# Low parts of the up-projection weights by an accumulating transfer instead of a VectorE subtraction, in a hybrid decoder layer on one core

## The chip, the cores and the metric

The kernel runs on one core of a Trainium2 chip. A core has a matrix engine (TensorE, PE in the profile; its weight loads are PEld), VectorE (DVE), ScalarE (ACT), GpSimd (POOL) and SyncE (SP), which here only issues transfers. Each engine works through its own list of instructions in order and waits on semaphores for the others. Sixteen DMA engines carry the transfers of all queues. On-chip data lie in SBUF (128 partitions), matmul results in PSUM (8 banks of 128 x 512 float32).

The metric is the device time of one execution in microseconds (us). The kernel before has a median of 772.62 us over 3 runs, from 772.52 to 773.3.

## The reference

One decoder layer on x of 512 x 1024, float32. Two attention branches (forgetting attention and stick-breaking attention, 8 heads each) are merged and projected; then comes a gated MLP with a causal convolution of width 3 between its up-projection and the gate. What the change touches is the up-projection of this second half:

```python
x = layer_norm(ALPHA * x + (1 + gt1) * attn_out, ln1_g, ln1_b)
u2 = x * (1 + sc2) + sh2
h = causal_depthwise_conv(u2 @ w_up, conv_w, conv_b)   # w_up: 1024 x 5632
h_gate, h_val = split(h, 2)
ffn_out = (silu(h_gate) * h_val) @ w_down              # w_down: 2816 x 1024
x = layer_norm(ALPHA * x + (1 + gt2) * ffn_out, ln2_g, ln2_b)
```

## The kernel before, in words

**Products in three parts.** TensorE is used with a reduced-precision float32 format (`F32R`). Each operand is split into a high part, the value rounded to that format, and a low part, the rounding error. A product is the sum of three matmuls: high x high, high weights x low activations, low weights x high activations (`mm3`, lines 110 to 112, in this order). The high part of a weight tile is a copy on ScalarE (`hi_of`, line 75, tile name `wh`), the low part is `raw - wh`, a subtraction on VectorE (`lo_of`, line 78, tile name `wl`).

**The stream of weight tiles.** All weights come as tiles of 128 x 1024 float32 (512 KB). `add_item` lists them with a function that prepares each; `weights(i)` issues the loads on SyncE's queue into four buffers called `raw`, up to three tiles ahead of i, and calls the preparing function up to two tiles ahead. For the up-projection that function is `split_proc` (line 143): it takes one of three `wh` and one of three `wl` buffers and makes the two parts. Four other kinds of tiles use the same four `raw` buffers: between the up tiles come 8 tiles `wa` of the conditioning weights, accumulated on VectorE (lines 524 and 529), and at the end the tiles `wdn` of the down-projection, which GpSimd first multiplies by the gate row `gt` (line 587).

**The up-projection.** Its 44 tiles are numbered n = 0 to 43 (gate and value columns alternate). For each, 8 groups of three matmuls fill one PSUM bank of 128 x 512. The first three tiles are done in two halves of 256 columns, because the second half of the activations is still being normalized. After a tile's matmuls ScalarE evacuates the bank with the convolution's last tap and bias (line 912, `cv`), VectorE adds the two other taps (lines 913, 914); after each odd tile ScalarE does the SiLU (line 919), VectorE the product (line 920), and the result is split into `hh` (ScalarE) and `hl` (VectorE).

**GpSimd during this stage.** From n = 6 on the code asks for `o_x1` (line 852), which finishes the first LayerNorm's output for the later residual: two rows are scaled by -0.5 (line 799, `lnr`) and 16 operations on 128 x 512 (lines 856 and 857, `xn`) multiply and add.

**What sets the order.** SyncE's instructions stand in the order of the program text. For the four other engines a scheduler orders the instructions when the kernel is built, by data dependences and by its own estimate of durations, and puts in the semaphore waits; on the chip each engine then keeps to its list.

Of the kernel before, what the change touches and what calls it, by code (L numbers as in the profile page):

```python
# [9 lines left out]
F32R = mybir.dt.float32r  # L10
BF16 = mybir.dt.bfloat16
AF = mybir.ActivationFunctionType
ALU = mybir.AluOpType
# [3 lines left out]
P = 128  # L17
# [18 lines left out]
WBUFS = 3  # L36
# [9 lines left out]
def layer_kernel(ctx: ExitStack, tc: tile.TileContext, out, xT, x, cT, crow, wa0, wa1, bcol, bgt, w1, wct, wv, bf,  # L46
# [3 lines left out]
    V, S, G, PE = nc.vector, nc.scalar, nc.gpsimd, nc.tensor  # L50

    cons = ctx.enter_context(tc.tile_pool(name="cons", bufs=1))
    stg = ctx.enter_context(tc.tile_pool(name="stg", bufs=1))
# [7 lines left out]
    def nm(s):  # L61
        cnt[0] += 1
        return f"{s}_{cnt[0]}"
# [7 lines left out]
    def fl(ap):  # L71
        return ap.bitcast(F32)

    def hi_of(o, i, scale=1.0):
        S.activation(o, i, AF.Copy, scale=scale)  # L75

    def lo_of(o, i, hi):
        return V.tensor_tensor(o, i, fl(hi), ALU.subtract)  # L78
# [39 lines left out]
    def add_item(src, proc, cols=1024):  # L118
        items.append([src, proc, cols, None, None])
        return len(items) - 1  # L120

    def weights(i, ahead=AHEAD):
        while state["load"] < min(len(items), i + LOADS):
            it = items[state["load"]]
            it[3] = stg.tile([P, 1024], F32, name=nm("raw"), tag="raw", bufs=LOADS)
            nc.sync.dma_start(it[3][:, 0 : it[2]], it[0])
            state["load"] += 1
            while state["proc"] <= state["load"] - LOADS:
                process()
        while state["proc"] < min(len(items), i + 1 + ahead):  # L130
            process()
        return items[i][4]
# [10 lines left out]
    def split_proc(r, cols=1024):  # L143
        h = stg.tile([P, 1024], F32R, name=nm("wh"), tag="wh", bufs=WBUFS)
        l = stg.tile([P, 1024], F32R, name=nm("wl"), tag="wl", bufs=WBUFS)
        hi_of(h[:, 0:cols], r[:, 0:cols])
        lo_of(l[:, 0:cols], r[:, 0:cols], h[:, 0:cols])
        return h, l


# [365 lines left out]
    def ada_proc(n):  # L516
        def f(r):
            if 8 <= n < 24:
                mod_col(2 + (n - 8) // 8, n % 8, r)
                return  # L520
            g, q = n // 4, n % 4
            if q == 0:
                ada_st[g] = z(F32, "ac2")
                V.tensor_scalar_mul(ada_st[g], r[:, 0:512], cTs[:, 0:1])
            acc = ada_st[g]
            for e in range(2):
                k = 2 * q + e
                if k > 0:
                    V.scalar_tensor_tensor(acc, r[:, e * 512 : (e + 1) * 512], cTs[:, k : k + 1], acc, ALU.mult, ALU.add)
        return f  # L530
# [54 lines left out]
    def wdn_proc(late):  # L585
        def f(r):
            G.tensor_tensor(r, r, gt[1], ALU.mult)  # L587
            if not late:
                h, l = split_proc(r)
                return [h[:, 0:512], h[:, 512:1024]], [l[:, 0:512], l[:, 512:1024]]  # L590
            h = [z(F32R, "wdh") for _ in range(2)]
            l = [z(F32R, "wdl") for _ in range(2)]
            for e in range(2):
                c = slice(e * 512, (e + 1) * 512)
                hi_of(h[e], r[:, c])
                lo_of(l[e], r[:, c], h[e])
            return h, l
        return f
# [20 lines left out]
    def add_proj(n, after):  # L619
        stream.append((proj, (add_item(wct[TILES.index(n)], split_proc), after)))  # L620
        flush_sum(len(stream))
# [7 lines left out]
    def add_bproj(br, j, after):  # L629
        if j % 2 == 0:  # L630
            wpi[br] = add_item(wp[br, j // 2], split_proc)
        stream.append((bproj, (br, j, wpi[br], after)))
# [227 lines left out]
    hh, hl = [], []  # L860
    wui, wai = [], {}
    for n in range(2 * FT):
        wui.append(add_item(wup[n], split_proc))
        if n % 4 == 3 and adas[0] < 32:
            add_item(wa1[adas[0]], ada_proc(adas[0]))
            wai[adas[0]] = len(items) - 1
            adas[0] += 1
# [27 lines left out]
    for n in range(2 * FT):  # L895
        if n < NSPLIT:
            h, l = items[wui[n]][4]
            ps = bks[n]
            up_mm(ps, h, l, slice(256, 512))
        else:  # L900
            ps = bank()
            h, l = weights(wui[n])
# [48 lines left out]
    for i in range(NB):  # L951
        tb = slice(i * P, (i + 1) * P)
        r = x1[i]
# [95 lines left out]
```

## The profile and times before

| | us |
|---|---|
| median of 3 runs | 772.62 |
| lowest, highest | 772.52, 773.3 |
| profiled execution, whole | 772.12 |
| its span in the trace | 770.3 |
| TensorE busy in the span | 748.1 (97%) |
| VectorE busy | 549.4 (71%) |
| ScalarE busy | 350.4 (45%) |
| GpSimd busy | 185.7 (24%) |
| up-projection, from the first matmul of tile 0 to the end of tile 43 | 400.2 to 642.4 |

The profile follows one execution. A row of a timeline gives start, duration, engine, line, operation, output and inputs, and in brackets how long the engine had been idle and who released it; a row with `x2` is two instructions merged. A row of groups gives after the bar the busy time, the mean duration in ns and the idle time before the instructions. A row of a window gives its length, then busy time and count of TensorE, weight loads, VectorE, ScalarE and GpSimd, then the granted clock, the DMA engines' share and GB/s. In the list of transfers the last number is the median time from issue to landing. Matmuls overlap in their pipeline, so each one's duration (0.39 us) is longer than the distance between two.

### The profile page before, as it was taken

Reading aid. Unit: us, or ns where it says so; the run is one execution under the profiler, and the core shown is the slowest. Engines: PE = TensorE matmul, PEld = TensorE weight load, DVE = VectorE, ACT = ScalarE, POOL = GpSimd, SP = SyncE. Lnnn points to the kernel's source line nnn. Section 1 sums busy time; section 2 is a strip of 40 time slices with the busy share of each in tenths; the row PEclk is TensorE's granted clock in tenths of the full one; section 3 lists DMA queues with packets and bytes.
Section 4 is the critical chain, followed back from the end, with each engine's and each line's share of the span. In section 5 each row is a group of like instructions: output and inputs, shape, how many; then the busy total and the mean of one; then the engine's idle time right before and its main releaser. Section 6 shows DMA issues by size and latency. Waiting matters only on the chain.

```text
span 770.3 us, 9560 instructions
## 1 busy us (share of the span) xinstructions
PE 748.1 (97%) x3556; PEld 620.6 (81%) x3556; DVE 549.4 (71%) x822; ACT 350.4 (45%) x583; POOL 185.7 (24%) x138
## 2 busy tenths in 40 slices
PE   5998999999999999999999999999999999999995
PEld 3886887788888888888889888888888888888885
DVE  6979889966687977776676787686656665533666
ACT  3357686717667556333145434444444433222400
POOL 1025424510000011364000780000000043945500
PEclk9999999999999999999999999999999999999998
DMA  8951253542333323455302524354332214323202
GB/s 310 403 204 55 83 165 131 175 161 83 110 110 110 127 93 136 144 190 164 137 1 73 201 79 145 118 177 137 114 105 93 100 55 165 120 98 127 65 28 83
DMA packets 31105, 99.68 MB, mean 129 GB/s; under 512 B 4273, under 2 KB 4785, under 8 KB 31058
## 3 DMA queue, kind: packets, MB, share of 16 engines
q1 hardware_dynamic: 30546, 99.00, 37.0%
q8 instruction: 28, 0.46, 0.2%
q14 instruction: 19, 0.16, 0.1%
q0 software_dynamic: 512, 0.07, 0.1%
HBM read 96.88 MB, written 2.10 MB: 128 GB/s over the span
## 4 chain that ended last, share of the span: by engine, by line
PE 86%; DVE 6%; ACT 5%; DMA 1%; issue 1%; SPq 0%; DVEq 0%; ACTq 0%
PE ps L110 17%; PE ps L111 17%; PE ps L112 17%; PE ps L941 5%; PE ps L940 5%; PE ps L942 5%; PE ps L254 4%; PE ps L495 2%; PE ps L821 2%; PE ps L820 2%; PE ps L819 2%; PE ps L477 2%; DVE om L456 1%; DMA wa<-in_wa 1%; ACT wh L75 1%
## 5 line engine op out<-in xcount | busy, mean ns | idle before, releaser
L78 DVE TENSOR_TENSOR wl<-raw,wh 128x1024 fp32r<-128x1024 f32 (+2 forms) x106 | 143.8, 1357 | 101.0 <-ACT wh L75 100.5
L75 ACT ACTIVATE wh<-raw 128x1024 fp32r<-128x1024 f32 (+2 forms) x106 | 110.4, 1042 | 108.1 <-PE ps L942 39.9
L110 PE MATMUL ps<-u2h,wh 128*128 128x512 f32 (+1 forms) x376 | 141.4, 376 | 0.0
L111 PE MATMUL ps<-u2l,wh 128*128 128x512 f32 (+1 forms) x376 | 141.2, 376 | 0.0
L112 PE MATMUL ps<-u2h,wl 128*128 128x512 f32 (+1 forms) x376 | 141.2, 375 | 0.0
L587 POOL TENSOR_TENSOR raw<-raw,gt 128x1024 f32<-128x1024 f32 x22 | 60.7, 2774 | 187.1 <-DVE gt L550 157.6
L110 PE MATMUL ps<-uh,wh 128*128 128x512 f32 x232 | 92.9, 400 | 2.2 <-DVE vv L78 2.2
L112 PE MATMUL ps<-uh,wl 128*128 128x512 f32 x232 | 90.8, 391 | 0.0
L111 PE MATMUL ps<-ul,wh 128*128 128x512 f32 x232 | 90.8, 391 | 0.0
L110 PEld LDWEIGHTS ps<-u2h,wh 128*128 128x128 f32 x376 | 70.8, 188 | 12.9
L111 PEld LDWEIGHTS ps<-u2l,wh 128*128 128x128 f32 x376 | 70.8, 188 | 12.8
L112 PEld LDWEIGHTS ps<-u2h,wl 128*128 128x128 f32 x376 | 70.8, 188 | 12.6
L110 PEld LDWEIGHTS ps<-uh,wh 128*128 128x128 f32 x232 | 43.6, 188 | 10.7 <-DVE vv L78 2.5
L112 PEld LDWEIGHTS ps<-uh,wl 128*128 128x128 f32 x232 | 43.6, 188 | 9.4
L111 PEld LDWEIGHTS ps<-ul,wh 128*128 128x128 f32 x232 | 43.7, 188 | 7.9
L940 PE MATMUL ps<-wh,hh 128*128 128x512 f32 x128 | 49.8, 389 | 0.0
L941 PE MATMUL ps<-wl,hh 128*128 128x512 f32 x128 | 49.8, 389 | 0.0
L942 PE MATMUL ps<-wh,hl 128*128 128x512 f32 x128 | 49.8, 389 | 0.0
L457 POOL TENSOR_TENSOR pt<-pt,om 128x127 f32<-128x127 f32 (+3 forms) x32 | 40.0, 1278 | 33.8 <-DVE om L456 28.7
L75 ACT ACTIVATE hh<-cv 128x512 fp32r<-128x512 f32 x22 | 13.9, 631 | 59.6 <-DVE cv L920 59.6
L575 POOL TENSOR_TENSOR raw<-raw,gt 128x1024 f32<-128x1024 f32 x8 | 21.1, 2645 | 78.0 <-DVE m L78 42.2
L919 ACT ACTIVATE cv<-cv 128x512 f32<-128x512 f32 x22 | 13.9, 632 | 54.5 <-DVE cv L914 54.5
(188 smaller groups left out, 1463.0 us busy)
## 6 DMA issues: line engine op xcount, KB each, us to landing
raw<-in_wup SPq DMA_DIRECT2D x44, 512.0 KB, 3.3
raw<-in_wa SPq DMA_DIRECT2D x32, 512.0 KB, 3.3
raw<-in_wct SPq DMA_DIRECT2D x29, 512.0 KB, 3.2
raw<-in_wdn SPq DMA_DIRECT2D x22, 512.0 KB, 3.2
wa<-in_wa SPq DMA_DIRECT2D x14, 512.0 KB, 8.7
raw<-in_wp SPq DMA_DIRECT2D x8, 512.0 KB, 3.3
raw<-in_wo SPq DMA_DIRECT2D x8, 512.0 KB, 3.6
raw<-in_w SPq DMA_DIRECT2D x7, 452.0 KB, 8.3
```

The costliest lines, as they stand in the source:

```text
L75: S.activation(o, i, AF.Copy, scale=scale)
L78: return V.tensor_tensor(o, i, fl(hi), ALU.subtract)
L110: PE.matmul(ps, wh, ah, start=first, stop=False)
L111: PE.matmul(ps, wh, al, start=False, stop=False)
L112: PE.matmul(ps, wl, ah, start=False, stop=last)
L254: PE.matmul(grp[g], w, u, start=j == 0 and n == 0, stop=j == KT - 1 and n == (1 if g == 7 else 2))
L457: G.tensor_tensor(pt[b][:, s : e - 1], pt[b][:, s : e - 1], om[:, s + 1 : e], ALU.mult)
L575: G.tensor_tensor(r, r, gt[0], ALU.mult)
L587: G.tensor_tensor(r, r, gt[1], ALU.mult)
L940: PE.matmul(ps, hh[j][:, tb], w[0], start=first, stop=False)
L941: PE.matmul(ps, hh[j][:, tb], w[1], start=False, stop=False)
L942: PE.matmul(ps, hl[j][:, tb], w[0], start=False, stop=last)
```

## The change

The 44 tiles of the up-projection are prepared by a new function, `split_dma`, in place of `split_proc`. ScalarE writes the negated high part into the `wl` buffer and the high part into the `wh` buffer, both from the raw tile. Then a transfer issued on GpSimd's queue adds the raw tile to what stands in `wl`, element by element, within SBUF. The result is `raw - high`, as before. VectorE's 44 subtractions are gone; ScalarE has 44 more copies, GpSimd's queue 44 transfers of 512 KB. A `raw` buffer of an up tile now comes free when the transfer has landed and the copies are done. TensorE's list and SyncE's list keep their order. All other tiles are split as before.

```diff
+    def split_dma(r):
+        h = stg.tile([P, 1024], F32R, name=nm("wh"), tag="wh", bufs=WBUFS)
+        l = stg.tile([P, 1024], F32R, name=nm("wl"), tag="wl", bufs=WBUFS)
+        hi_of(l, r, -1.0)
+        hi_of(h, r)
+        G.dma_start(fl(l), r, accum_op=ALU.add)
+        return h, l
...
     for n in range(2 * FT):
-        wui.append(add_item(wup[n], split_proc))
+        wui.append(add_item(wup[n], split_dma))
```

## The prediction

> **What bounds the kernel now.** I read the page's busy shares and chain first, then the windows of the up projection, the groups of instructions in that window, and at last the timelines of single engines.
>
> ```profile
> PE 748.1 (97%) x3556; PEld 620.6 (81%) x3556; DVE 549.4 (71%) x822; ACT 350.4 (45%) x583; POOL 185.7 (24%) x138
> PE 86%; DVE 6%; ACT 5%; DMA 1%; issue 1%; SPq 0%; DVEq 0%; ACTq 0%
> ...
> 400.20:418.40 18.20, 18.20 (x156) 18.20 (x154) 11.65 (x26) 9.89 (x18) 0.00 (x0) 1.00 0.09 30
> 418.40:642.40 224.00, 224.00 (x990) 185.45 (x989) 161.26 (x187) 96.50 (x128) 37.43 (x21) 1.00 0.35 118
> ...
> L112 PE MATMUL ps<-u2h,wl 128*128 128x512 f32 (+1 forms) x329 | 127.9, 389 | 0.0
> L78 DVE TENSOR_TENSOR wl<-raw,wh 128x1024 fp32r<-128x1024 f32 x41 | 56.8, 1384 | 43.7 <-ACT wh L75 43.6
> L75 ACT ACTIVATE wh<-raw 128x1024 fp32r<-128x1024 f32 x41 | 43.1, 1053 | 15.5 <-PE ps L111 15.5
> L912 ACT ACTIVATE cv<-ps,cw 128x512 f32<-128x512 f32 x41 | 31.2, 760 | 0.8 <-PE ps L112 0.8
> ```
>
> The up projection lasts from 400.2 to 642.4 us. In both its windows TensorE (first pair after the commas) is busy for the whole length, and the matmuls that read the low parts, `wl`, were preceded by 0.0 us of idle time. The VectorE work that the change takes away, 41 of its 44 subtractions here with 56.8 us, stands beside a full TensorE. So removing it can gain nothing: the lower bound of that term is zero, not a gain. The question is only whether the new way of making `wl` is ever late.
>
> **When a low part is needed.** I number the 44 weight tiles 0 to 43; step n is the 24 matmuls of tile n.
>
> ```profile
> 412.72 1.06 ACT L75 ACTIVATE wh<-raw 128x1024 fp32r<-128x1024 f32 x1 [3.37 <-PE ps L111]
> 413.68 0.76 ACT L912 ACTIVATE cv<-ps,cw 128x512 f32<-128x512 f32 x1
> 415.60 1.06 ACT L75 ACTIVATE wh<-raw 128x1024 fp32r<-128x1024 f32 x1 [1.15 <-PE ps L111]
> ...
> 417.34 1.28 ACT L919 ACT_TABLE_LOAD   x1
> 418.63 0.63 ACT L919 ACTIVATE cv<-cv 128x512 f32<-128x512 f32 x1
> ...
> 418.40 0.40 PE L110 MATMUL ps<-u2h,wh 128*128 128x512 f32 x1
> ...
> 423.84 1.06 ACT L75 ACTIVATE wh<-raw 128x1024 fp32r<-128x1024 f32 x1 [2.35 <-PE ps L111]
> ...
> 429.28 1.07 ACT L75 ACTIVATE wh<-raw 128x1024 fp32r<-128x1024 f32 x1 [3.19 <-PE ps L111]
> ```
>
> The last two rows are ScalarE let go by the ends of steps 3 and 4: a step is 5.44 us, a matmul 0.227 us. Step 3 begins at 418.40, step n at 418.40 + 5.44(n-3). The third matmul of a step is the first to read `wl`, 0.46 us in. There are three `wl` buffers, so tile n's is written from the end of step n-3 and read two steps later.
>
> In the changed kernel's instruction order ScalarE does, per tile, high part, evacuation of step n-3, negated copy. By the rows (starts 0.96 apart, the evacuation some 0.7, the copy 1.04) the copy ends 2.7 us after step n-3 does. From there the transfer has 10.88 + 0.46 - 2.7 = 8.6 us in the steady state. ScalarE's extra 44 copies (44 x 1.05 = 46 us) fit: 1.05 + 0.76 + 1.05 us and half of the two 0.63 us operations of each pair of tiles make 3.5 of 5.44 us. That and the raw loads, which now wait for a transfer's landing, I cost at nothing: with four raw buffers a load has more than a step before its use.
>
> **The price of one accumulating transfer**, from the end of the copy to its landing, is L. The trace has none of this size on GpSimd's queue.
>
> ```profile
> q1 hardware_dynamic: 30546, 99.00, 37.0%
> ...
> raw<-in_wup SPq DMA_DIRECT2D x44, 512.0 KB, 3.3
> wa<-in_wa SPq DMA_DIRECT2D x14, 512.0 KB, 8.7
> ...
> m<-chi POOLq DMA_DIRECT2D x8, 4.0 KB, 1.6
> ...
> L327 POOL DMA_DIRECT2D m<-chi x8 | 4.3, 534 | 0.6 <-POOL m L325 0.6
> ```
>
> Bounds: a plain load of the same size lands in 3.3 us; crowded loads at the kernel's start in 8.7 us. Between them: 99.00 MB held 16 engines for 37.0% of 770.3 us, 285 us, so 512 KB hold them 1.51 us. An accumulation reads raw and `wl`: 3.0 us. With 0.53 us of issue and the 1.6 us that even 4 KB take, L = 5.2 us. I take that, since it uses the only rows of GpSimd's queue, and keep 3.3 and 8.7. By the Trainium skill (DMA: Bandwidth & Descriptors, Anatomy of one DMA) a GpSimd transfer costs about 2.0 us + bytes/436e3, 3.2 us here, which the plain load's 3.3 us agrees with; by Collectives: The Full Stack (The bandwidth ceiling) a reduction reads two sources at twice the traffic, so an estimate of 4.4 us, with which the sum below would give 784.0 us. No run here shows it yet.
>
> **Step 3, the shortest notice.** Its buffer comes free at 412.6 us, but the half steps before it are short. High part, evacuation and copy end at 415.4; `wl` is due at 418.86. Stall: L - 3.46 = 1.7 us (0 at 3.3, 5.2 at 8.7). Tile 4's copy comes behind the table load and the operation after it (until 419.2): it ends at 420.2, landing 425.4, due 424.3 + 1.7: hidden.
>
> **Step 9, behind GpSimd's own work.** This is the main term. GpSimd runs its list in order, and a transfer issued there waits its turn and makes others wait. The changed kernel's list (line numbers 8 higher than in the profile) reads, shortened:
>
> ```
> DMACopy wl of tile 8     [waits Activation]
> L807 lnr; L864 xn; L807 lnr; L864; L865; L864; L865; L865; L864; L864; L865; L865; L864
> DMACopy wl of tile 9
> L865 xn
> DMACopy wl of tile 10
> L864; L864; L865; L865
> DMACopy wl of tile 11
> ```
>
> These are the 18 operations that finish x1 after the first LayerNorm. Before, they ran freely:
>
> ```profile
> 429.18 1.76 POOL L799 TENSOR_SCALAR lnr<-lnr 128x512 f32<-128x512 f32 x1 [62.08 <-DMA lnr<-in_lnrow]
> 431.03 1.71 POOL L856 TENSOR_TENSOR xn<-xn,lnr 128x512 f32<-128x512 f32 x1
> ...
> 434.61 1.28 POOL L856 TENSOR_TENSOR xn<-xn,lnr 128x512 f32<-128x512 f32 x1
> 435.86 1.29 POOL L857 TENSOR_TENSOR xn<-xn,lnr 128x512 f32<-128x512 f32 x1
> 437.12 2.27 POOL L856 TENSOR_TENSOR xn<-xn,lnr 128x512 f32<-128x512 f32 x1
> ...
> 447.77 3.52 POOL L856 TENSOR_TENSOR xn<-xn,lnr 128x512 f32<-128x512 f32 x2
> ...
> 436.45 1.79 DVE L78 TENSOR_TENSOR wl<-raw,wh 128x1024 fp32r<-128x1024 f32 x1 [1.71 <-ACT wh L75]
> ```
>
> The thirteen ahead of tile 9 lasted from 429.18 to the middle of the last POOL row, 449.5: 20.3 us. An undisturbed one takes 1.28 us, one that met VectorE's `wl` subtraction 2.27. Those subtractions are gone, other two-operand work stays: I take 18.5 us, between 13 x 1.28 = 16.7 and 20.3. They now stand behind tile 8's transfer, which waits for the copy after step 5: 434.72 + 2.7 = 437.4, issue 0.55. So tile 9's transfer is issued at 437.4 + 0.55 + 18.5 = 456.45 (plus the 1.7 of step 3, which moves the need too), lands 5.2 later, and was due at 451.50. Stall: 10.15 us, or L + 4.95. Tile 10 is issued at 458.3, lands by 465, due 467.1; tile 11 at about 464, due 472.5 against 469: hidden in that stall.
>
> TensorE then restarts after about 10 us without work. The only such restart in the trace:
>
> ```profile
> 10.46 1.65 PE L254 MATMUL ps<-uh,wh 128*128 128x512 f32 x3 [6.18 <-ACT uh L227]
> ...
> 13.89 0.62 PE L254 MATMUL ps<-wl,uh 128*128 128x512 f32 x2
> 14.35 0.84 PE L254 MATMUL ps<-ul,wh 128*128 128x512 f32 x3
> ```
>
> After 6.18 us of idling eight matmuls took 13.89 - 10.46 = 3.43 us, and the next two 0.46: 0.43 us each instead of 0.23, so 1.6 us lost. I add 1.6.
>
> **The two ends of the stage.** Tiles 0 to 2 are split while the attention branches are merged; the last of their transfers stands behind GpSimd's last merge addition (first row), so it is issued at about 367 us and needed from 400.18: nothing. At the end GpSimd's multiplications of the first down weights stand between the transfers of tiles 41 to 43.
>
> ```profile
> 364.90 2.20 POOL L675 TENSOR_TENSOR sg<-sg,sg 128x512 f32<-128x512 f32 x1 [2.07 <-DVE sg L569]
> ...
> 400.18 0.36 PE L110 MATMUL ps<-u2h,wh 128*128 128x256 f32 x1
> ...
> L587 POOL TENSOR_TENSOR raw<-raw,gt 128x1024 f32<-128x1024 f32 x22 | 60.7, 2774 | 187.1 <-DVE gt L550 157.6 <-DMA raw<-in_wdn 29.5
> ```
>
> Such a multiplication needs a raw tile loaded into the buffer that tile 40's transfer frees: landing at 2.7 + L after the end of step 37, load 3.3, multiplication 2.77: 8.8 + L. Tile 42's transfer follows it and is due 22.2 us after that point. 8.8 + 2L is 19.2 at L = 5.2: hidden by 3 us; at 8.7 it is 26.2, a stall of 4.0 us.
>
> **Sum.** 1.7 + 10.15 + 1.6 = 13.5 us, or 2L + 3.1. The profiled execution took 772.12 us (span 770.3 and 1.8 around it): 785.6 us. The median of the runs, 772.62, lies 0.5 above it; the difference is within the range. At L = 3.3 step 3's stall is gone: 8.25 + 1.6, 782.0. At 8.7: 20.5, 4.0 at the end, another 1.6 for a restart after step 3: 798.
>
> **Rivals.** First, the DMA engines become the bound. If read, read and write each take 1.51 us, a transfer holds them 4.5 us; with 52 loads on 44 steps (1.8 us a step) that is 6.3 of 5.44 us. For it: nothing in the trace accumulates. Against: a plain copy also reads and writes in its 1.51 us. Over 41 steps 0.9 us each is 37 us, with the stalls at L = 6.7 (16.5 us) less what they share, about 50: 822 us. Second, on the other side, no change: the transfers do not wait behind GpSimd's arithmetic, but are taken by its sequencer as SP's are, and L is the plain load's 3.3. Then tile 9's copy, behind the evacuation of step 7 at 445.6 us, ends at 447.4, lands at 450.7 and is in time for 451.5: 772.1 us. It decides as soon as L is under 3.46; at 5.2 it leaves 1.7 + 1.1, 775.0. Against it: the two transfers of the forget gate's rows are listed among GpSimd's instructions with 0.53 us each. Third, that the copy and addition don't make the same low part can't change the time; no instruction depends on values.
>
> **How the numbers follow.** The forecast's case, in-order GpSimd and L between 3.3 and 8.7, has 0.78, 782 to 798 us; saturation 0.14; overtaking 0.08, half of it within 0.2%, a quarter faster by some overlap I do not see, a quarter slower. 0.2% is about what a measurement of this kernel can tell from no change. Predicted 785.6 us; the range 777 to 815 leaves out the last rival and the upper part of saturation. Faster 0.02, the same 0.04, slower 0.94.
>
> **What would show it.** Right: a wait of TensorE on a DMA into `wl` of about 10 us near 453 us and one below 3 us near 419, none between 475 and 630; GpSimd's thirteen operations starting near 440, followed by the transfer; a median time to landing of 5 us in the list of DMA issues; VectorE less by about 60 us, ScalarE more by 46. Wrong: waits of TensorE on `wl` at every step (L over 8.6), or no long one near 453 (order of GpSimd's work not binding), or the DMA share above 0.9 through the stage.

## The result, and the profile after

The changed kernel takes 791.03 us (median of four runs, 788.43 to 791.31) against 772.71 us for the kernel before on the same chip: a ratio of 1.0228, with a 95% interval of 1.0206 to 1.025, so slower by 18.3 us. The profiled execution took 791.31 us with a span of 789.5 us, 19.2 us longer than before's 770.3.

The page of the changed kernel (line numbers from line 150 on are 8 higher than before): busy times, the chain's shares by engine, two groups of instructions (busy and mean ns of one, then idle time ahead and its releaser), the two large DMA queues (packets, MB, share of 16 engines), and the median time to landing of the two transfers per weight tile.

```profile
PE 756.7 (96%) x3556; PEld 624.8 (79%) x3556; DVE 505.6 (64%) x778; ACT 393.2 (50%) x627; POOL 216.9 (27%) x182
...
PE 78%; issue 6%; DVE 5%; DMA 4%; ACT 3%; POOL 2%; SPq 0%; DVEq 0%; POOLq 0%; ACTq 0%
...
L112 PE MATMUL ps<-u2h,wl 128*128 128x512 f32 (+1 forms) x376 | 144.0, 383 | 11.9 <-DMA wl<-raw 11.8
...
L155 POOL DMA_DIRECT2D wl<-raw x44 | 39.1, 889 | 217.9 <-ACT wl L75 166.2
...
q1 hardware_dynamic: 30546, 99.00, 35.7%
q0 software_dynamic: 6848, 23.14, 16.4%
...
raw<-in_wup SPq DMA_DIRECT2D x44, 512.0 KB, 5.2
wl<-raw POOLq DMA_DIRECT2D x44, 512.0 KB, 6.0
```

The matmuls that read the low parts had no idle time ahead of them before; now they have 11.9 us, nearly all of it waiting for the transfer into `wl`. VectorE's busy time fell from 549.4 to 505.6 us, ScalarE's rose from 350.4 to 393.2, and TensorE gained nothing by it. The DMA's share of the chain rose from 1% to 4%. The transfers hold the 16 DMA engines for 16.4% of 789.5 us; over 44 that is 2.94 us each, where a plain load of the same size holds them 1.51 us.

TensorE's timeline gives the places. These six rows are all its waits over 0.5 us in the stage (start, duration, then in brackets the idle time just before and what ended it):

```profile
420.96 0.50 PE L112 MATMUL ps<-u2h,wl 128*128 128x512 f32 x1 [1.24 <-DMA wl<-raw]
427.31 0.50 PE L112 MATMUL ps<-u2h,wl 128*128 128x512 f32 x1 [0.63 <-DMA wl<-raw]
446.46 0.79 PE L112 MATMUL ps<-u2h,wl 128*128 128x512 f32 x1 [2.54 <-DMA wl<-raw]
464.48 0.80 PE L112 MATMUL ps<-u2h,wl 128*128 128x512 f32 x1 [5.47 <-DMA wl<-raw]
545.08 0.51 PE L112 MATMUL ps<-u2h,wl 128*128 128x512 f32 x1 [1.10 <-DMA wl<-raw]
573.75 0.50 PE L112 MATMUL ps<-u2h,wl 128*128 128x512 f32 x1 [0.81 <-DMA wl<-raw]
```

Each is the third matmul of a step: of steps 3, 4, 7, 9, 23 and 28. Counted as what each gap between two starts is over the pitch of 0.227 us, which takes in the first slow matmul after a gap, the steps lost 1.5, 0.9, 2.7, 5.6 and, from step 23 on with four gaps under 0.25 us and their restarts, 3.2 us. Steps 7 and 9 also lose 1.4 and 2.6 us because the matmuls behind them run at 0.43 us each. The windows just after step 9's wait show that clock (the number behind POOL's bracket; the next is the DMA share):

```profile
464.00:466.00 2.00, 1.52 (x4) 1.25 (x5) 2.00 (x1) 0.00 (x0) 2.00 (x4) 0.50 1.09 205
466.00:468.00 2.00, 2.00 (x6) 1.59 (x5) 2.00 (x1) 0.00 (x0) 2.00 (x3) 0.50 0.98 291
```

The sum is 17.9 us; all gaps of the stage together are 18.4 us larger than before. The stage also began 0.7 us later; why is not known, and among the traces of all runs its start varies from 400.2 to 402.7 us.

Three places of the other engines tell why steps 7 and 9 were late: GpSimd around them, and the queue of SyncE.

```profile
431.60 3.21 SPq L804 DMA_DIRECT2D lnr<-in_lnrow  x4
...
435.37 0.86 POOL L155 DMA_DIRECT2D wl<-raw  x1 [4.99 <-ACT wl L75]
440.81 0.86 POOL L155 DMA_DIRECT2D wl<-raw  x1 [4.58 <-ACT wl L75]
441.38 1.85 POOL L807 TENSOR_SCALAR lnr<-lnr 128x512 f32<-128x512 f32 x1
...
458.13 1.72 POOL L864 TENSOR_TENSOR xn<-xn,lnr 128x512 f32<-128x512 f32 x1
459.81 0.89 POOL L155 DMA_DIRECT2D wl<-raw  x1
...
DMA to landing us min/median/max: 4.5/6.0/11.0
```

GpSimd issued tile 8's transfer at 440.81, then worked through thirteen operations of the residual from 441.38 to 459.8, and issued tile 9's only then; it landed 4.7 us later, at TensorE's 464.48. That is the wait the prediction was built on. Tile 7's transfer, by contrast, was issued early, at 435.37, and landed 11.0 us later, the longest of all (last row). Just ahead of it, at 431.60 to 434.81, SyncE had issued the four row loads of the residual (`lnr`, 256 KB each).

The late waits, from step 23 on, begin at another load. First the kernel before, then the changed kernel: SyncE, VectorE, ScalarE and GpSimd ahead of step 23.

```profile
511.16 1.54 DVE L529 SCALAR_TENSOR_TENSOR ac<-raw,cTs,ac 128x512 f32<-128x512 f32 x2 [0.67 <-DMA raw<-in_wa]
...
524.88 0.38 SPq L126 DMA_DIRECT2D raw<-in_wa  x1
...
532.73 1.54 DVE L537 SCALAR_TENSOR_TENSOR ac<-raw,cTs,ac 128x512 f32<-128x512 f32 x2 [8.33 <-DMA raw<-in_wa]
...
536.47 0.63 ACT L75 ACTIVATE hh<-cv 128x512 fp32r<-128x512 f32 x1 [7.26 <-DVE cv L928]
...
540.48 0.86 POOL L155 DMA_DIRECT2D wl<-raw  x1 [10.11 <-ACT wl L75]
```

The load is a conditioning tile `wa`, which comes behind tile 23 and takes the `raw` buffer of tile 20. It was issued 0.5 us after tile 20's transfer had landed, and it took 7.8 us to land beside the transfers, where in the kernel before it took 3.2. VectorE waited 8.33 us for it, and the convolution of an earlier tile waited in VectorE's list behind it. ScalarE's list has the split of that result ahead of tile 23's parts, so ScalarE waited 7.26 us for VectorE, and tile 23's transfer was issued at 540.48 and not near 535, where the pace of the transfers before it would have put it. The same chain of waits stands ahead of steps 27 and 28 (VectorE waits 6.11 us) and of steps 31 and 32 (7.15 us). In the whole stage VectorE waited 28.3 us for these loads, against 1.1 us before.

### The profile page after: what moved, and what is told of

Same layout as the page of the kernel before. It is cut to its first block, busy times and chain, and to the rows that moved or that the text cites. A ratio compares the mean times of both kernels' runs of the same rounds, so it can differ in the third digit from the quotient of the medians.

```text
span 789.5 us, 9686 instructions
## 1 busy us (share of the span) xinstructions
PE 756.7 (96%) x3556; PEld 624.8 (79%) x3556; DVE 505.6 (64%) x778; ACT 393.2 (50%) x627; POOL 216.9 (27%) x182
## 3 DMA queue, kind: packets, MB, share of 16 engines
q0 software_dynamic: 6848, 23.14, 16.4%
## 4 chain that ended last, share of the span: by engine, by line
PE 78%; issue 6%; DVE 5%; DMA 4%; ACT 3%; POOL 2%; SPq 0%; DVEq 0%; POOLq 0%; ACTq 0%
PE ps L112 14%; PE ps L110 14%; PE ps L111 14%; PE ps L262 6%; PE ps L949 5%; PE ps L948 5%; PE ps L950 5%; DMA wl<-raw 3%; PE ps L503 2%; PE ps L485 2%; PE ps L828 2%; PE ps L827 2%; PE ps L829 2%; PE ps L428 1%; DVE om L464 1%
## 5 line engine op out<-in xcount | busy, mean ns | idle before, releaser
L112 PE MATMUL ps<-u2h,wl 128*128 128x512 f32 (+1 forms) x376 | 144.0, 383 | 11.9 <-DMA wl<-raw 11.8
L110 PE MATMUL ps<-u2h,wh 128*128 128x512 f32 (+1 forms) x376 | 143.0, 380 | 0.0
L78 DVE TENSOR_TENSOR wl<-raw,wh 128x1024 fp32r<-128x1024 f32 (+3 forms) x62 | 85.7, 1384 | 51.0 <-ACT wh L75 50.5
L155 POOL DMA_DIRECT2D wl<-raw x44 | 39.1, 889 | 217.9 <-ACT wl L75 166.2
L921 DVE SCALAR_TENSOR_TENSOR cv<-ps,cw,cv 128x511 f32<-128x511 f32 x44 | 32.9, 748 | 77.8 <-ACT cv L920 77.8
L595 POOL TENSOR_TENSOR raw<-raw,gt 128x1024 f32<-128x1024 f32 x22 | 59.6, 2722 | 39.1 <-DMA raw<-in_wdn 39.1
L537 DVE SCALAR_TENSOR_TENSOR ac<-raw,cTs,ac 128x512 f32<-128x512 f32 x28 | 30.3, 1083 | 29.7 <-DMA raw<-in_wa 29.3
```

The source lines that it names most:

```text
L110: PE.matmul(ps, wh, ah, start=first, stop=False)
L112: PE.matmul(ps, wl, ah, start=False, stop=last)
L155: G.dma_start(fl(l), r, accum_op=ALU.add)
```

## Experiments

The theory after the result: four separate things make `wl` late. (1) GpSimd's list (step 9); (2) the row loads in front of tile 7's transfer; (3) little look-ahead, because a tile's `wl` buffer comes free only two steps before the step that uses it (steps 3 and 4, and the late waits, where ScalarE's copy is late too); (4) under all of it the doubled price of a transfer that adds. The main rival: transfers at this pace are too much for the DMA engines, and the rest only decides where it shows. The kernel before, measured beside the first four runs, took 772.61 us, and beside the last four 773.41 us.

**The residual on VectorE.**

```
 ln_row:  -  G.tensor_scalar(t[e], t[e], -0.5, None, ALU.mult)
          +  V.tensor_scalar(t[e], t[e], -0.5, None, ALU.mult)
 o_x1:    -  G.tensor_tensor(x1[i][e], x1[i][e], lnr[0][e], ALU.mult)      # and the ALU.add below it
          +  V.tensor_tensor(x1[i][e], x1[i][e], lnr[0][e], ALU.mult)
```

> The eighteen operations of the residual (two scalings of the rows and sixteen products and sums) are moved from GpSimd to VectorE; the row loads stay where they are. Theory: step 9 waits (5.47 us on TensorE, and about 2.6 us of matmuls at half clock behind it) because GpSimd works through 18.5 us of these operations before it can issue tile 9's transfer. Then step 9's wait falls under 0.5 us, step 7's wait of about 2.5 us stays, and the time falls by about 8 us to 783 us (782 to 785). Rival: the transfers as such are too slow for the pace, GpSimd's list only decides which step shows it. Then what step 9 loses comes back at steps 8 to 12 and the time stays at 789 us or more.

Measured: 783.64 us, a ratio of 1.0136 (1.0116 to 1.0157). TensorE's two longest waits of the stage, and the instructions ahead of the second one on ScalarE and GpSimd:

```profile
447.22 0.79 PE L112 MATMUL ps<-u2h,wl 128*128 128x512 f32 x1 [2.40 <-DMA wl<-raw]
461.31 0.50 PE L112 MATMUL ps<-u2h,wl 128*128 128x512 f32 x1 [1.34 <-DMA wl<-raw]
...
454.12 0.78 ACT L920 ACTIVATE cv<-ps,cw 128x512 f32<-128x512 f32 x1 [8.94 <-PE ps L112]
...
455.32 1.05 ACT L75 ACTIVATE wl<-raw 128x1024 fp32r<-128x1024 f32 x1
...
456.66 0.86 POOL L155 DMA_DIRECT2D wl<-raw  x1 [14.10 <-ACT wl L75]
```

The time fell as GpSimd's list said, and step 9's wait and its half-clock matmuls went with it; nothing like the 7 us came back at later steps. The rival falls for this part. One point of the expectation missed: step 9 keeps 1.34 us and not under 0.5. Its negated copy stands in ScalarE's list behind an evacuation that waits for the end of step 7, which step 7's own wait had put off; the transfer went at 456.66 and landed as TensorE's wait ended. Step 7's wait is as before.

**And the row loads ahead of the stage.** On top of that edit:

```
+    lnr.extend([ln_row(0), ln_row(1)])
     weights(wui[0], 0)
     bks = [bank() for n in range(NSPLIT)]
```

> As the run with the residual on VectorE, and the four row loads (256 KB each) are issued ahead of the up projection's fourth weight tile, before the stage, and not behind step 6. Theory: tile 7's transfer landed 11.0 us after its issue because the four row loads filled the DMA engines just ahead of it. Then step 7's wait of 2.5 us and its restart of about 1.4 us go as well: 779 us (777 to 781), with the longest landing of a transfer below 9 us. Rival: tile 7's transfer is held up by the loads of the raw tiles or by its own queue. Then its wait stays and the time is that of the run with the residual on VectorE alone, 783 us.

Measured: 779.62 us, 1.0086 (1.0071 to 1.0102). TensorE at steps 3 and 4 and at the largest later wait, the group of its `wl` matmuls, and the landing of the transfers:

```profile
420.50 0.50 PE L112 MATMUL ps<-u2h,wl 128*128 128x512 f32 x1 [1.22 <-DMA wl<-raw]
426.65 0.50 PE L112 MATMUL ps<-u2h,wl 128*128 128x512 f32 x1 [0.41 <-DMA wl<-raw]
577.48 0.50 PE L112 MATMUL ps<-u2h,wl 128*128 128x512 f32 x1 [0.76 <-DMA wl<-raw]
...
L112 PE MATMUL ps<-u2h,wl 128*128 128x512 f32 (+1 forms) x376 | 142.7, 380 | 3.2 <-DMA wl<-raw 3.2
...
DMA to landing us min/median/max: 4.5/5.9/8.8
```

Steps 7 and 9 no longer wait, no matmul runs at half clock, and the longest landing is 8.8 us. The raw loads and the transfers' own queue are the same in both runs, so it was the row loads that held up tile 7, whose transfer now lands 5.3 us after its issue.

**The first twelve tiles as before, 32 by the transfer.**

```
-        wui.append(add_item(wup[n], split_dma))
+        wui.append(add_item(wup[n], split_dma if n >= 12 else split_proc))
```

> The first twelve weight tiles are split as before (VectorE subtracts), the other 32 by the transfer. Theory: the start of the stage costs about 15 us and the steady pace about 3 us, in waits of up to 1 us where the DMA engines are over 0.83 busy. Then the waits at steps 3, 4, 7 and 9 are gone, those between 540 and 600 us stay, and the time is 775.5 us (773.5 to 778). Rival: the late waits are what is left of the disturbed start, and a stage that starts undisturbed has none: 772.7 us, as the kernel before.

Measured: 779.02 us, 1.008 (1.0065 to 1.0095): above the expected 775.5, outside its range. The loss is not where I looked. TensorE at the first two steps whose tiles come by transfer, then ScalarE and GpSimd ahead of the first:

```profile
471.81 0.50 PE L112 MATMUL ps<-u2h,wl 128*128 128x512 f32 x1 [1.93 <-DMA wl<-raw]
479.34 0.50 PE L112 MATMUL ps<-u2h,wl 128*128 128x512 f32 x1 [1.80 <-DMA wl<-raw]
...
463.67 0.63 ACT L927 ACTIVATE cv<-cv 128x512 f32<-128x512 f32 x1 [7.66 <-DVE cv L922]
464.21 1.04 ACT L75 ACTIVATE wh<-raw 128x1024 fp32r<-128x1024 f32 x1
465.15 0.76 ACT L920 ACTIVATE cv<-ps,cw 128x512 f32<-128x512 f32 x1
465.82 1.04 ACT L75 ACTIVATE wl<-raw 128x1024 fp32r<-128x1024 f32 x1
...
467.17 0.95 POOL L155 DMA_DIRECT2D wl<-raw  x1 [6.66 <-ACT wl L75]
```

The change of method at tile 12 costs 4.3 us, gaps and slow first matmuls together. GpSimd was free from 460.5 on; it is ScalarE that comes late, because its list put the negated copy behind an operation that waited 7.66 us for VectorE, which still carried the old subtractions. After that, only two waits of 0.5 us remain, 1.3 us in all, where the changed kernel loses 3.2 us. So the steady pace costs between 1.3 and 3.2 us in these two traces, and the rival, which had no late waits at all, falls too. Whether the difference comes from the changed kernel's disturbed start is not shown: the run with the row loads ahead of the stage, whose steps 7 and 9 do not wait, still loses 3.3 us from step 11 on.

**The first twelve tiles by the transfer, the others as before** (the condition the other way round).

> The first twelve weight tiles by the transfer, the other 32 as before. Theory: the start (steps 3, 4, 7 and 9 with the two restarts) is nearly all of the loss: 772.6 + 1.5 + 0.9 + 4.1 + 8.2 = 787.3 us (785.5 to 789). Rival, by the run with the last 32 tiles by the transfer, which lost 6.4 us: the two parts add up to the whole, and this one costs 18.4 - 6.4 = 12 us, 784.6 us; that needs step 9's wait to be 2.7 us shorter than in the changed kernel.

Measured: 788.99 us, 1.0204 (1.0189 to 1.0219), 15.6 us above before: the theory's 787.3 is nearer than the rival's 784.6, which falls. Step 9's wait is as in the changed kernel:

```profile
464.08 0.80 PE L112 MATMUL ps<-u2h,wl 128*128 128x512 f32 x1 [5.40 <-DMA wl<-raw]
```

The loss of this run, 15.6 us, and that of the run with 32 tiles by the transfer, 6.4 us, add up to more than the changed kernel's 18.3, since the 4.3 us at the change of method occur in the latter alone.

**A transfer that only copies.**

```
-        G.dma_start(fl(l), r, accum_op=ALU.add)
+        G.dma_start(fl(l), r)
```

> The addition is left out: the transfer copies the raw tile over ScalarE's negated part, so the low part is wrong, but every wait, issue and buffer is as in the changed kernel. Theory: it is the accumulation that makes a packet take 328 ns in place of 159 ns and the landing 6.0 us. Then the queue's share falls from 16.4% to about 8%, the landing's median to about 4 us, the waits at steps 3 and 4 and the late ones go, those at steps 7 and 9 shrink by 1 to 2 us each: 782 us (779 to 785). Rival: the price is that of a transfer issued by GpSimd from one SBUF tile to another, with or without the addition: 789 to 791 us and packets of 300 ns and over.

Measured: 785.12 us, 1.0152 (1.0134 to 1.0171), just above the expected range. The queue, GpSimd's issue, the landing, and TensorE's one long wait:

```profile
q0 software_dynamic: 6848, 23.14, 7.6%
...
L155 POOL DMA_DIRECT2D wl<-raw x44 | 23.7, 539 | 230.1 <-ACT wl L75 181.2
...
DMA to landing us min/median/max: 2.8/3.1/8.0
...
462.79 0.80 PE L112 MATMUL ps<-u2h,wl 128*128 128x512 f32 x1 [8.28 <-DMA wl<-raw]
```

The addition is the price: with it the same 23.14 MB take 16.4% of the engines and not 7.6%, an issue takes 889 ns and not 539, a landing 6.0 us and not 3.1. The median packet of 4096 B of these transfers is 336 ns with it and 162 ns without (the 328 ns of the expectation is the commonest value, 159 ns the median of the loads). That the engines' time about doubles agrees with what the Trainium skill says of a reduction in collectives, which reads two sources (Collectives: The Full Stack, The bandwidth ceiling). By the Trainium skill (DMA: Bandwidth & Descriptors, Anatomy of one DMA) a transfer of this size from GpSimd would take an estimated 2.0 us + bytes/436e3, 3.2 us, which agrees with the copy's 3.1 us and not with the accumulation's 6.0. The waits at steps 3 and 4, at step 7 and after step 9 are gone. Step 9's is longer, 8.28 us, though the landing is shorter: no earlier wait puts off TensorE's need, and GpSimd reaches tile 9's transfer at the same point of the trace, 459.8 us. That is the miss of the expectation, which had step 9's wait shrink with the landing.

**No transfer at all** (the same line removed).

> The transfer is left out: ScalarE writes the high part and the negated high part, nothing adds the raw tile, so the low part is wrong; GpSimd's list and the row loads are as in the changed kernel. Theory: ScalarE's second copy costs nothing by itself: no wait of TensorE over 0.3 us in the up projection, 772.6 us (772.0 to 773.5). Rival: part of the loss at steps 3 and 4 is ScalarE's list, where the negated copy stands behind an evacuation and a table load: then waits of 0.5 us and more stay there, now for ScalarE, and the time is 774 us or more.

Measured: 772.8 us, 0.9994 (0.9985 to 1.0004). ScalarE's 44 additional copies and GpSimd's list cost nothing, and the time without VectorE's subtractions is that of before. The group of the `wl` matmuls:

```profile
L112 PE MATMUL ps<-u2h,wl 128*128 128x512 f32 (+1 forms) x376 | 141.2, 375 | 0.0
```

**The two moves in the kernel before.** The residual on VectorE and the row loads ahead of the stage, with `split_proc` for every tile.

> The kernel before, without the transfer, with the same two moves as the run of the residual on VectorE and the row loads ahead of the stage. Theory: both moves are neutral where VectorE makes the low parts: 772.6 us (772.0 to 773.5), so that the distance of the changed kernel with these moves is the transfer's own. Rival: VectorE, with 18 operations more, delays the low parts or the evacuations: 774 us or more, with waits of TensorE for VectorE at steps 8 to 13.

Measured: 772.84 us, 0.9996 (0.9986 to 1.0005). The moves are neutral by themselves, so what they saved in the changed kernel they saved for the transfers.

**A fourth buffer for the low parts.** On top of the two moves, in the changed kernel:

```
-NZ = 60
+NZ = 59
-        l = stg.tile([P, 1024], F32R, name=nm("wl"), tag="wl", bufs=WBUFS)
+        l = stg.tile([P, 1024], F32R, name=nm("wl"), tag="wl", bufs=WBUFS + 1)      # the same in the two other functions that take a wl buffer
```

> As the run with the residual on VectorE and the row loads ahead of the stage, with a fourth buffer for the low parts (and 59 in place of 60 of the small activation tiles, to make room for it). Theory: what that run still loses, 7 us, comes from the look-ahead: the negated copy for step n cannot be written before the last matmul of step n-3, and copy, issue and landing then take longer than the two steps left whenever ScalarE's list or the DMA engines are late. With the fourth buffer the waits at steps 3 and 4 (1.4 and 0.6 us) and the late ones go: 773.5 us (772.5 to 775.5). Rival: the DMA engines cannot carry raw loads and transfers at this pace, and an earlier start only lengthens the queue. Then the landing's median rises above 7 us and the time stays at 778 us or more.

Measured: 774.47 us, 1.002 (1.0009 to 1.003). The group of the `wl` matmuls, the queue, the landing, and the stage in one window (TensorE's busy time is the first number after the comma, its clock and the DMA share stand behind POOL):

```profile
L112 PE MATMUL ps<-u2h,wl 128*128 128x512 f32 (+1 forms) x376 | 141.1, 375 | 0.0
...
q0 software_dynamic: 6848, 23.14, 16.4%
...
DMA to landing us min/median/max: 4.5/5.7/8.4
...
420.00:643.00 223.00, 223.00 (x986) 184.56 (x985) 108.89 (x148) 132.50 (x166) 40.77 (x42) 1.00 0.84 207
```

With the DMA engines busy for 0.84 of this window and 39 of the 44 transfers issued in it, TensorE has no idle time. VectorE still waits for the `wa` loads, 35.6 us in six waits, but the step of notice more takes up the delay. The rival that the engines cannot carry the transfers falls: they can, if the copy may be written a step earlier. Of the changed kernel's loss, as ratios, 1.0228 went to 1.0136 (GpSimd's list), 1.0086 (row loads) and 1.002 (look-ahead). Of the last 0.2%, 1.1 us, the profile shows 0.5 us: gaps near 411 us, ahead of this window, where TensorE waits for VectorE's low part of the activations (`u2l`). The rest was not found. Whether the late waits also go when the `wa` loads are moved was not tried. No variant beats the kernel before: its TensorE never waited for a low part, so there was nothing to win.

## Why the prediction was right, and where its terms were off

The forecast was slower, 785.6 us; it came out slower, 791.03 us, inside the range and 5.4 us above the number. Step by step:

- *Removing VectorE's subtractions gains nothing.* Right, and shown: the run without a transfer stays within 0.1% of before.
- *The price of one transfer.* The engines' time was put at 3.0 us and measured 2.94. The landing was one number, 5.2 us from the end of the copy. It is not one number: from the issue, which stands 0.3 us behind the copy's end, it is 4.5 us at least, 6.0 in the median and 11.0 beside the row loads. The issue was taken as 0.53 us from GpSimd's small transfers; it is 0.89 us with an addition and 0.54 without.
- *Step 3, 1.7 us.* Measured 1.5.
- *Tile 4 hidden.* Wrong by 0.9 us. The margin was 0.6 us, and two transfers ran at once there (issues at 421.2 and 422.7), so this landing took 6.1 us from the issue.
- *Step 9, L + 4.95 = 10.15 us.* The mechanism was right: the copy-only run, whose L is near 3.1, should wait 8.05 us by this formula and waits 8.28. The list of thirteen operations was put at 18.5 us and took 18.4 (441.38 to 459.81). The wait itself was 5.6 us and not 10.15, because step 7's wait and slow matmuls, 4.1 us, had put off TensorE's need by as much; together they are 9.8 us. The unforeseen wait at step 7 hence added little to the whole, but it is a cause of its own, as the 4.0 us it was worth once GpSimd's list was gone show.
- *What was missed at step 7.* The prediction priced the transfer alone and the raw loads beside it, and did not ask what else SyncE would send in front of it. The row loads are rows of the trace of before (`lnr` there starts GpSimd's list); they were used for GpSimd and not for the DMA engines.
- *Restart, 1.6 us.* Measured 2.6 us behind step 9 and 1.4 us behind step 7, the latter made up for by step 9's shorter wait. One restart in the trace of before was too little to size another: after the same idling of about 6 us at the kernel's start, the slow matmuls lasted from 3.0 to 6.0 us in the ten traces.
- *Steady pace and raw loads at nothing.* This is the largest miss of the sum: 3.2 us. "A load has more than a step before its use" fails for the `wa` loads: their buffer came free later and they landed later, VectorE waited up to 8.33 us for one, and through VectorE and ScalarE the copy of a low part came some 5.5 us late. The transfer's 8.6 us hold only if that copy is on time. The run with the fourth buffer shows that notice is enough to remove these waits, at the same load of the DMA engines.
- *VectorE less by about 60 us, ScalarE more by 46.* ScalarE's 43 us fit. VectorE's 44 us do not: 44 subtractions are gone, as said, and the subtractions' own durations fell by 58 us, but the multiply-adds of the `wa` tiles took 7.2 us longer, most of it in one of 7.9 us at 460 us; the rest was not followed. This lies off TensorE's path.
- *The end of the stage hidden.* Right, but closer than forecast: no wait at tiles 41 to 43, and tile 42's transfer, issued 3.6 us behind its copy because of GpSimd's multiplications, landed 0.6 us ahead of its use, where 3 us were left by the sum.
- *The signs.* GpSimd's operations came near 440 us and the wait below 3 us near 419, as said. The wait of about 10 us near 453 came in two, 2.5 us at 446 and 5.5 us at 464, and "none between 475 and 630" failed, with two waits over 0.5 us.
- *Rivals.* Saturation (822 us) did not occur; the DMA engines' share from 420 to 650 us was 0.83. Overtaking did not: GpSimd's transfers wait their turn.

In terms of the sum: 13.5 predicted; -0.2 (step 3), +0.9 (step 4), -0.4 (steps 7 and 9 with step 7's slow matmuls against 10.15), +1.0 (restart) and +3.2 (late waits) give 18.0 us.

## What to carry to other kernels

Work taken off an engine that the bound engine never waits for saves nothing, so the new way can only cost; ask first how late it may be. A transfer put on an engine's queue inherits that engine's list: look for the longest run of other work in it, and for large loads on other queues just ahead of it. When a longer path is taken into a pipeline, give it one more buffer: here 0.6% hung on a single tile of notice. And when a buffer of a shared ring comes free later, follow every load that uses the ring, not only those that were changed: here the `wa` tiles, prepared as before, carried the delay on.

## What the runs showed of the hardware

- An accumulating SBUF to SBUF transfer of 512 KB holds the 16 DMA engines 2.94 us, a median of 336 ns per 4096 B packet against 162 ns of a copy, and costs GpSimd 0.89 us of issue against 0.54.
- With four broadcast loads of 256 KB issued on SyncE's queue within 3.2 us just ahead of it, one such transfer landed after 11.0 us, and after 5.3 us when these loads were moved ahead of the stage. I had not expected this of another queue.
- The granted clock fell to 0.50 for a while around the end of some waits: for 3.4 us at the wait of 2.5 us (step 7), 6.8 us at that of 5.5 us (step 9) and 10.2 us, in part still idle, at the copy-only run's 8.3 us; matmuls then ran at 0.43 us each. At the 1.9 us of the run with 32 tiles by transfer it did not fall.
- The length of the wait alone does not decide this: near 66 us TensorE idles 2.2 to 2.3 us in every trace, and the clock then fell to 0.50 for 3.4 us in the changed kernel's trace and not at all in that of the kernel before.
